# Decay sums of a gated linear attention: tokens on partitions and triangles on TensorE in place of scans on VectorE

## The chip, the core and the metric

The kernel runs on one core of a Trainium2 chip. The metric is the device time of one execution in microseconds; the number of a version is the median of its runs. The core has TensorE (matrix products, output to PSUM), VectorE, ScalarE and GpSimd for elementwise work, and a sync queue that issues most transfers. Each engine takes its instructions in a fixed order and waits at an instruction until its operands are there.

## The reference

One layer of a hybrid block: a modulated norm, one input projection for two groups of heads, an output projection and a SwiGLU feed-forward part. 2048 latent tokens and 256 context tokens, width 1024. The change is in group B, gated linear attention (GLA): 4 heads, 64 decay values a head, two directions. The decay of a token comes from a low-rank input of 16 values, a bias, a log-sigmoid and a division by 16; what the attention uses is its running sum within a chunk.

```python
loga = [log_sigmoid((glr[..., i * 16:(i + 1) * 16] @ g_gate_w[i] + g_gate_b[i])) / G_TAU for i in range(2)]
...
def step(S, inp):                                  # one chunk of gla_scan
    qc, kc, vc, ac = inp
    bcum = jnp.cumsum(ac, -2)                      # running sum of the decays
    decay = where(lower, bcum[..., :, None, :] - bcum[..., None, :, :], NEG)
    att = einsum('bhtk,bhsk,bhtsk->bhts', qc, kc, exp(decay))
    out = einsum('bhtk,bhkv->bhtv', qc * exp(bcum), S) + einsum('bhts,bhsv->bhtv', att, vc)
```

The second direction does the same on the flipped sequence. The kernel works with chunks of 128 tokens, for which the sums restart.

## The kernel before

**Stages.** All data are float32; most products are made in a fast float32 type (fp32r) with operands split in two parts. A main stream of units (projections: gates, keys and queries, values; then convolutions, output gates; then output projection and feed-forward part) is written out unit by unit. After each of its steps `after_step` advances the tasks: decays (`bt_task`, kind b), GLA (`scan_ga`, `state_g`, `scan_g`, kind g), mLSTM (`m_tables`, `state_m`, `scan_m`, kind m). A task is a generator; a `yield n` ends what it emits in this step.

**What sets the order.** For kinds b, g and m, tasks are advanced only while VectorE isn't more than a limit behind TensorE in a small model (`load.behind() > lim[0]`); it adds a fixed cost and a cost per column to each engine as instructions are emitted. A scheduler with its own timeline then fixes the order of each engine. A change of costs in one place so moves instructions elsewhere.

**A decay task.** `bt_task` handles 256 tokens for all four heads; there are nine (eight half blocks and the context). It loads the low-rank input three times (parts of a split), rounds it to fp32r (`glr`, 98 rows with the bias rows), and multiplies: for each head weights `w2[:, cs(h)]` are stationary and `glr` moves. The result `zh[h]` has 128 partitions (64 decays of the forward direction, 64 of the backward) and 256 tokens. Abs, Exp and Ln on ScalarE and a minimum-and-subtract on VectorE give the log-sigmoid. Two `tensor_tensor_scan` on VectorE for each head give the sums, on partitions 0 to 63 forwards and on 64 to 127 backwards, with a mask `rmask` that restarts the sum every 128 tokens. The result is stored to `d_bt` and loaded again by the GLA tasks, which turn it into factors (`dec` in `gla_e`, the levels in `gla_att`).

**Names.** `take()` hands out buffers of 128x256 named `arena`; `PS()` takes one of the four PSUM banks `ps`; `mm` are the four banks of the main stream; `gm` are five buffers of 128x512; `xall` holds the keys of the decay levels. `d_bg` and `d_mp` are small tables of `m_tables` that go through memory; `area` in ScalarE's rows of this stage is weight data of the modulation (`in_wada`).

## Time and profile before

| | us |
|---|---|
| median of 3 runs | 2954.2 (2951.46 to 2954.33) |
| profiled execution | 2949.42 |
| its span, first to last instruction | 2947.6 |
| TensorE busy | 2656.3 |
| VectorE busy | 1946.4 |
| GpSimd busy | 1781.4 |
| ScalarE busy | 1389.2 |

The mean granted clock of TensorE is 0.946 of full speed. The nine decay tasks run between 100 and 550 us, beside the input projections; the output projection and the feed-forward part follow from about 1400 us. Busy time is a mean over the span; the rows further down give it by stretches. A row's "idle before" and a wait name the operation that ended the idle time. Times in microseconds count from the start of the span.

### The profile page before, as it was taken

The numbers are of one execution on the slowest core, as the hardware profiler recorded it, in microseconds if no ns is written. First come the engines' busy times: TensorE is split into PE (matmuls) and PEld (weight loads), VectorE is DVE, ScalarE is ACT, GpSimd is POOL, SyncE is SP. The second block draws the span as 40 slices with busy tenths as digits, with TensorE's granted clock in tenths as the row PEclk, the third lists the DMA queues.
The fourth block names the chain that finished last, engine by engine and source line by source line (L and its number), as shares of the span: only waits on it lengthen the run. The fifth ranks groups of instructions, "written<-read, shape, count | busy, mean of one in ns | idle before, by whom it ended". The sixth has DMA issues, their size and how long they took to land. (4 is left out here: it accounts for less than half of the span.)

```text
span 2947.6 us, 43643 instructions
## 1 busy us (share of the span) xinstructions
PE 2656.3 (90%) x13322; PEld 2225.2 (75%) x13322; DVE 1946.4 (66%) x3949; ACT 1389.2 (47%) x3307; POOL 1781.4 (60%) x2339
## 2 busy tenths in 40 slices
PE   7889998698999977897999999889997999998898
PEld 4778887587777766775878888677786888886677
DVE  7678889886973435778778644767657444447775
ACT  4565555435455555655565433434434333333343
POOL 5767643345555534766767555777766655557773
PEclk8989899899999998997999999999998999999999
DMA  6755533246576776752443422422572432224222
GB/s 260 235 168 172 163 110 116 67 140 193 179 218 200 202 210 208 236 181 67 149 134 105 155 86 79 142 69 76 176 250 89 131 106 79 83 76 145 75 63 86
DMA packets 292458, 418.40 MB, mean 142 GB/s; under 512 B 38270, under 2 KB 176798, under 8 KB 289536
## 3 DMA queue, kind: packets, MB, share of 16 engines
q1 hardware_dynamic: 284864, 397.42, 43.4%
q0 software_dynamic: 7360, 18.19, 1.8%
q8 instruction: 106, 1.74, 0.3%
q14 instruction: 128, 1.05, 0.1%
HBM read 304.99 MB, written 110.49 MB: 141 GB/s over the span
## 5 line engine op out<-in xcount | busy, mean ns | idle before, releaser
L194 PE MATMUL mm<-area,w 128*128 128x512 f32 (+2 forms) x8264 | 1997.0, 399 | 119.2 <-DVE area L194 41.3
L194 PEld LDWEIGHTS mm<-area,w 128*128 128x128 f32 (+1 forms) x8264 | 1559.5, 193 | 465.2 <-DVE area L194 44.4
L194 POOL TENSOR_TENSOR w<-area,w 128x256 fp32r<-128x256 f32 x572 | 452.7, 814 | 295.6 <-ACT w L194 277.0
L194 POOL TENSOR_TENSOR w<-wr,w 128x256 fp32r<-128x256 f32 (+2 forms) x484 | 408.9, 865 | 205.7 <-ACT w L194 182.4
L194 POOL TENSOR_TENSOR arena<-arena 128x128 f32<-128x128 f32 (+1 forms) x520 | 245.5, 496 | 163.2 <-DMA arena<-d_bt 44.3
L194 ACT CAST w<-area 128x512 fp32r<-128x512 f32 x286 | 176.9, 620 | 285.7 <-PE mm L194 259.8
L194 PE MATMUL ps<-arena,arena 128*128 128x129 f32 (+1 forms) x1420 | 214.0, 292 | 58.8 <-ACT arena L194 29.5
L194 PEld LDWEIGHTS ps<-arena,arena 128*128 128x128 f32 x1420 | 193.6, 203 | 82.7 <-ACT arena L194 37.9
L194 PE MATMUL mm<-w,area 128*128 128x256 f32 x1728 | 245.6, 299 | 6.0 <-ACT gm L194 4.7
L194 DVE SCALAR_TENSOR_TENSOR gm<-gm,pc 128x63 f32<-128x63 f32 (+5 forms) x408 | 233.0, 613 | 7.2 <-ACT gm L194 4.8
L194 DVE TENSOR_TENSOR area<-area 128x512 f32<-128x512 f32 (+2 forms) x230 | 169.2, 749 | 100.6 <-DMA area<-in_wgu_dram 52.5
L194 PEld LDWEIGHTS mm<-w,area 128*128 128x128 f32 x1728 | 229.9, 204 | 7.7 <-ACT gm L194 4.9
L194 ACT CAST w<-wr 128x512 fp32r<-128x512 f32 (+3 forms) x272 | 158.1, 584 | 143.7 <-PE mm L194 62.9
L194 DVE TENSOR_TENSOR arena<-ps,arena 64x128 f32<-64x128 f32 (+1 forms) x512 | 154.9, 303 | 81.4 <-ACT ps L194 56.3
L194 DVE TENSOR_TENSOR gm<-mm,gm 128x512 f32<-128x512 f32 (+3 forms) x136 | 93.1, 684 | 159.0 <-PE mm L194 137.4
L194 ACT COPY gm<-mm 128x512 f32<-128x512 f32 (+3 forms) x215 | 123.2, 575 | 148.5 <-PE mm L194 128.1
L194 DVE SCALAR_TENSOR_TENSOR area<-mm,modc,area 128x512 f32<-128x512 f32 (+1 forms) x184 | 132.0, 722 | 92.0 <-PE mm L194 91.8
L194 ACT ACTIVATE ps<-arena 128x256 f32<-128x256 f32 x224 | 84.8, 383 | 157.4 <-DVE xall L194 106.4
L194 DVE TENSOR_TENSOR arena<-arena,arena 128x256 f32<-128x256 f32 (+2 forms) x146 | 117.1, 812 | 57.5 <-ACT arena L194 36.9
L194 PEld LDWEIGHTS ps<-arena,xall 128*128 128x128 f32 x896 | 125.6, 209 | 38.1 <-DVE arena L194 10.8
L194 PE MATMUL ps<-arena,xall 128*128 128x64 f32 x896 | 131.6, 289 | 24.4 <-DVE arena L194 13.1
L194 DVE TENSOR_TENSOR xall<-ps,arena 64x128 f32<-64x128 f32 x448 | 129.3, 289 | 6.9
(177 smaller groups left out, 3083.0 us busy)
## 6 DMA issues: line engine op xcount, KB each, us to landing
area<-in_wgu_dram SPq DMA_DIRECT2D x170, 256.0 KB, 2.7
d_ff<-gm SPq DMA_DIRECT2D x88, 256.0 KB, 2.0
arena<-d_ff SPq DMA_DIRECT2D x88, 256.0 KB, 2.8
wr<-in_win_dram SPq DMA_DIRECT2D x72, 256.0 KB, 3.6
area<-in_wada_dram SPq DMA_DIRECT2D x32, 512.0 KB, 4.6
wr<-in_wout_dram SPq DMA_DIRECT2D x64, 256.0 KB, 3.6
arena<-d_kq SPq DMA_DIRECT2D x112, 128.0 KB, 2.9
arena<-d_bt SPq DMA_DIRECT2D x80, 128.0 KB, 3.3
```

What stands on the lines that cost most here:

```text
L194: return f(out, *args, **kw)
```

## The change

The projection has its operands exchanged: a chunk of 128 tokens of `glr` is stationary and all 512 columns of `w2` move, so tokens stand on partitions and decays in columns. Abs, Exp, Ln and the subtraction are the same in number and shape. After one more step (`YB3`), each chunk, head and direction has a product with a triangle of ones: the 64 decays are stationary (128 tokens by 64), the triangle `tri` moves, and the output is again decays by tokens, 64x128, for the backward direction in partitions 64 to 127 and with -1. These products are in full float32. ScalarE copies the sums out of PSUM. The mask's place is taken by the two triangles.

```diff
-YB, YB2, YN, YGB = 1, 1, 1, 1
+YB, YB2, YB3, YN, YGB = 1, 1, 1, 1, 1
...
-    rm = np.ones((P, HB), np.float32)
-    rm[:, ::P] = 0
-    o["rmask"] = rm
+    o["tri"] = np.concatenate([np.triu(np.ones((P, P), np.float32)), -np.tril(np.ones((P, P), np.float32))], 1)
...
-    rmask = take()
-    dma(rmask, I["rmask"])
+    tri = take()
+    dma(tri, I["tri"])
...
         zs = [PS() for _ in range(2)]
-        for h in range(NH):
-            PE.matmul(zs[h // 2][:, h % 2 * HB:h % 2 * HB + HB], w2[:, cs(h)], glr, start=True, stop=True)
+        for c in range(2):
+            PE.matmul(zs[c], glr[:, cs(c)], w2, start=True, stop=True)
         ms = [take() for h in range(NH)]
-        zh = [zs[h // 2][:, h % 2 * HB:h % 2 * HB + HB] for h in range(NH)]
+        zh = [zs[i // 2][:, i % 2 * HB:i % 2 * HB + HB] for i in range(NH)]
...
         for h in range(NH):
-            m = o = ms[h]
-            V.scalar_tensor_tensor(m, zh[h], 0.0, m, ALU.min, ALU.subtract)
-            V.tensor_tensor_scan(o[0:64], rmask[0:64], m[0:64], 0.0, ALU.mult, ALU.add)
-            V.tensor_tensor_scan(o[64:128][:, ::-1], rmask[64:128], m[64:128][:, ::-1], 0.0, ALU.mult, ALU.subtract)
+            V.scalar_tensor_tensor(ms[h], zh[h], 0.0, ms[h], ALU.min, ALU.subtract)
+        yield YB3
+        os = [PS() for _ in range(2)]
+        for h in range(NH):
+            for c in range(2):
+                for d in range(2):
+                    PE.matmul(os[h // 2][64 * d:64 * d + 64, h % 2 * HB + c * P:h % 2 * HB + c * P + P],
+                              ms[2 * c + h // 2][:, h % 2 * P + 64 * d:h % 2 * P + 64 * d + 64], tri[:, cs(d)], start=True, stop=True)
+        free(*ms)
+        for h in range(NH):
+            o = take()
+            S.copy(o, os[h // 2][:, h % 2 * HB:h % 2 * HB + HB])
             dma(dst(h), o)
             free(o)
```

The order of the instructions changes too, and not only inside the tasks. On TensorE, at the second decay task, the projection was in four products (output `ps`, moving `gm`, weights `arena_329` as printed: output, then operands), between projections of keys and queries (`mm`):

```order
L194 MATMUL ps<-gm,arena_329 128x256 x2
L194 MATMUL mm<-area_471,w 128x512 x2
L194 MATMUL mm<-area_472,w 128x512 x12
L194 MATMUL mm<-area_553,w 128x512 x5
L194 MATMUL ps<-gm,arena_329 128x256 x2
L194 MATMUL ps<-arena_89,xall 128x64 x4
L194 MATMUL mm<-area_553,w 128x512 x7
L194 MATMUL mm<-area_554,w 128x512 x9
L194 MATMUL ps<-ones,area_814 128x2
```

and is now, in two products, followed by main stream and then by the first of the task's sixteen triangles (`arena_81` is `tri`, `arena_93` and `arena_94` are the decays):

```order
L192 MATMUL ps<-ones,area_814 128x2
L192 MATMUL ps<-arena_329,gm 128x512 x2
L192 MATMUL ps<-arena_91,xall 128x64 x4
L192 MATMUL mm<-area_297,w 128x256 x23
L192 MATMUL mm<-area_471,w 128x512 x12
L192 MATMUL mm<-area_472,w 128x512
L192 MATMUL ps<-ones,area_814 128x2
L192 MATMUL mm<-area_472,w 128x512 x11
L192 MATMUL mm<-area_553,w 128x512 x6
L192 MATMUL ps<-ones,area_814 128x2
L192 MATMUL mm<-area_553,w 128x512 x3
L192 MATMUL ps<-arena_81,arena_93 64x128 x2
```

The projection has become half as many products of twice the width; 56 products of the main stream and a level (`xall`) stand between it and the first triangle, and seven more pairs of triangles follow that row, of arena_94 and arena_93 in turn.

On VectorE, at the same task, the four subtractions (output and operands 128x256) and the scans (64x256, printed with the same operation's name; `arena_81` is the mask) were:

```order
L194 SCALAR_TENSOR_TENSOR arena_91<-ps,arena_91 128x256 x2
L194 SCALAR_TENSOR_TENSOR arena_91<-arena_81,arena_91 64x256 x2
L194 SCALAR_TENSOR_TENSOR arena_92<-ps,arena_92 128x256
L194 SCALAR_TENSOR_TENSOR arena_91<-arena_81,arena_91 64x256 x2
L194 SCALAR_TENSOR_TENSOR arena_92<-ps,arena_92 128x256
L194 TENSOR_SCALAR modc<-ps,pc 128x2
L194 TENSOR_TENSOR area_814<-area_814 128x256
L194 TENSOR_TENSOR arena_94<-ps,arena_88 64x128 x2
L194 SCALAR_TENSOR_TENSOR arena_92<-arena_81,arena_92 64x256 x2
L194 TENSOR_TENSOR xall<-ps,arena_87 64x32x4 x2
```

and are now:

```order
L192 TENSOR_TENSOR arena_95<-ps,arena_90 64x128 x2
L192 TENSOR_TENSOR xall<-ps,arena_89 64x16x8 x2
L192 SCALAR_TENSOR_TENSOR arena_93<-ps,arena_93 128x256
L192 TENSOR_TENSOR area_814<-area_814 128x128
L192 SCALAR_TENSOR_TENSOR arena_93<-ps,arena_93 128x256
L192 SCALAR_TENSOR_TENSOR arena_94<-ps,arena_94 128x256 x2
L192 TENSOR_SCALAR modc<-ps,pc 128x2
L192 TENSOR_TENSOR area_814<-area_814 128x256
L192 TENSOR_TENSOR area_814<-area_814 128x128
```

The eight scans of the task are gone; the additions of the modulation weights (`area_814`) and the multiplications of the levels (`xall`) come closer together.

On the sync queue, at the small table `d_bg` of `m_tables`, the order was:

```order
L210 DMA d_bt<-arena_85 128x256 x2
L208 DMA arena_85<-d_kq 128x256
L210 DMA d_bg<-sm_6006 128x2x1
L208 DMA arena_89<-d_bt 128x256
L208 DMA arena_90<-d_bg 4x2x16 x2
L210 DMA d_qT<-gm 128x512
L210 DMA d_mp<-arena_90 4x2x16 x2
L208 DMA sm_6024<-d_mp 128x2x1
L208 DMA mpb<-d_mp 128x128
```

and is now:

```order
L208 DMA d_kq<-gm 64x2x256
L208 DMA d_bg<-sm_6128 128x2x1
L208 DMA d_kq<-gm 64x2x256 x2
L206 DMA arena_82<-d_bg 4x2x16 x2
L208 DMA d_kq<-gm 64x2x256
L206 DMA arena_95<-d_gv 128x256
L206 DMA arena_86<-d_us 64x256
L208 DMA d_kq<-gm 64x2x256 x2
L208 DMA d_att<-arena_83 128x256
L208 DMA d_mp<-arena_82 4x2x16
```

The load of decays (`d_bt`) that stood between the store and the loads of `d_bg` has moved ahead of this place; stores of keys and queries (`d_kq`) and loads for the GLA state (`d_gv`, `d_us`) stand there instead, and the table comes at a later state of GLA.

## Rows read from the trace of the kernel before

**Rows 1.** The page, section 1: busy time, share of the span, instructions

```profile
span 2947.6 us, 43643 instructions
...
PE 2656.3 (90%) x13322; PEld 2225.2 (75%) x13322; DVE 1946.4 (66%) x3949; ACT 1389.2 (47%) x3307; POOL 1781.4 (60%) x2339
```

**Rows 2.** Busy time by stretches; columns: stretch, length, engines, clock, DMA

```profile
core 0: us, PE busy (x) PEld busy (x) DVE busy (x) ACT busy (x) POOL busy (x), PEclk, DMA share, GB/s
...
100.00:300.00 200.00, 175.40 (x1174) 164.01 (x1172) 155.63 (x385) 121.25 (x306) 147.08 (x208) 0.91 0.59 186
300.00:400.00 100.00, 90.69 (x614) 83.79 (x615) 86.22 (x229) 57.28 (x129) 56.87 (x106) 0.88 0.50 153
400.00:550.00 150.00, 137.44 (x804) 121.41 (x803) 132.34 (x309) 82.93 (x177) 58.84 (x100) 0.97 0.34 103
...
860.00:1100.00 240.00, 216.22 (x1125) 180.11 (x1124) 89.55 (x262) 119.68 (x387) 120.93 (x194) 0.97 0.70 206
```

**Rows 3.** Groups of VectorE: count, busy us, mean ns, idle before

```profile
L194 DVE TENSOR_TENSOR_SCAN arena<-arena,arena 64x256 f32<-64x256 f32 x70 | 60.0, 857 | 0.8
L194 DVE TENSOR_TENSOR_SCAN arena<-arena 64x256 f32<-64x256 f32 x2 | 1.4, 703 | 0.0
```

**Rows 4.** TensorE's waits, 100 to 300 us: total, times, longest us

```profile
PE ps L194 <- DVE arena L194: 7.5, 4, 3.7
...
PE ps L194 <- DVE xall L194: 2.1, 4, 0.8
...
PE ps L194 <- DVE gm L194: 1.2, 1, 1.2
```

**Rows 5.** TensorE's waits, 300 to 400 us

```profile
PE ps L194 <- DVE arena L194: 4.0, 2, 2.5
PE mm L194 <- DVE area L194: 3.6, 2, 3.3
...
PE ps L194 <- DVE gm L194: 0.6, 1, 0.6
```

**Rows 6.** TensorE's waits, 400 to 550 us

```profile
PE ps L194 <- DVE xall L194: 5.4, 4, 2.4
PE mm L194 <- ACT gm L194: 4.7, 1, 4.7
```

**Rows 7.** Timeline of all engines, 553 to 567 us: start, us, engine, instruction

```profile
553.38 0.37 SPq L210 DMA_DIRECT2D d_bg<-sm  x1
...
553.84 0.42 SPq L208 DMA_DIRECT2D arena<-d_bt  x1
...
562.87 0.66 SPq L208 DMA_DIRECT2D arena<-d_bg  x2
...
565.93 0.42 ACT L194 ACTIVATE dec<-arena 64x2 f32<-64x2 f32 x2 [10.48 <-DMA arena<-d_bt]
...
566.21 0.24 DVE L194 TENSOR_TENSOR_SCAN arena<-arena,mctx 4x16 f32<-4x16 f32 x1 [9.45 <-DMA arena<-d_bg]
...
566.96 0.58 ACT L194 COPY gm<-mm 128x512 f32<-128x512 f32 x1
567.12 7.82 PE L194 MATMUL mm<-area,w 128*128 128x512 f32 x24 [15.54 <-ACT gm L194]
```

**Rows 8.** Groups of TensorE over the whole span

```profile
L194 PE MATMUL mm<-area,w 128*128 128x512 f32 x7992 | 1946.1, 401 | 109.4 <-DVE area L194 37.7 <-ACT gm L194 20.1 <-ACT area L194 18.3
...
L194 PE MATMUL mm<-w,area 128*128 128x256 f32 x1728 | 245.6, 299 | 6.0 <-ACT gm L194 4.7 <-POOL w L194 1.2
...
L194 PE MATMUL ps<-gm,arena 98*128 98x256 f32 x36 | 6.8, 296 | 2.4 <-DVE gm L194 2.0 <-DVE xall L194 0.3
```

**Rows 9.** Groups of TensorE: the products of the decay levels

```profile
L194 PE MATMUL ps<-arena,xall 128*128 128x64 f32 x896 | 131.6, 289 | 24.4 <-DVE arena L194 13.1 <-DVE xall L194 8.4 <-DVE gm L194 1.5
```

**Rows 10.** Timeline of TensorE, 1011 to 1015 us

```profile
1011.45 2.40 PE L194 MATMUL ps<-arena,arena 128*128 128x129 f32 x20
1013.61 1.41 PE L194 MATMUL mm<-area,w 128*128 128x512 f32 x5
```

**Rows 11.** Groups of TensorE, 100 to 300 us

```profile
L194 PE MATMUL ps<-arena,xall 128*128 128x64 f32 x172 | 27.0, 303 | 4.1 <-DVE arena L194 2.7 <-DVE xall L194 1.0
```

**Rows 12.** Groups of TensorE, 400 to 550 us

```profile
L194 PE MATMUL ps<-arena,xall 128*128 128x64 f32 x116 | 16.0, 274 | 6.1 <-DVE xall L194 5.4 <-DVE arena L194 0.4 <-issue 0.3
```

**Rows 13.** Groups of ScalarE over the whole span

```profile
L194 ACT ACT_TABLE_LOAD x33 | 42.3, 1283 | 1.3 <-PEq L2149 0.7
...
L194 ACT COPY arena<-ps 128x256 f32<-128x256 f32 x104 | 37.9, 370 | 21.9 <-DVE arena L194 15.7 <-PE ps L194 6.0
```

**Rows 14.** Timeline of ScalarE, 226 to 234 us

```profile
226.42 0.65 ACT L194 ACTIVATE arena<-ps 128x256 f32<-128x256 f32 x2
226.95 1.27 ACT L194 ACTIVATE area<-area,cx 128x128 f32<-128x128 f32 x4
...
230.39 0.42 ACT L194 ACTIVATE arena<-arena 128x256 f32<-128x256 f32 x1
230.83 1.28 ACT L194 ACT_TABLE_LOAD   x1
232.13 0.73 ACT L194 ACTIVATE arena<-arena 128x256 f32<-128x256 f32 x2
...
233.01 0.72 ACT L194 ACTIVATE arena<-arena 128x256 f32<-128x256 f32 x2
```

**Rows 15.** Busy time by stretches of 20 us (columns as in rows 2)

```profile
460.00:480.00 20.00, 14.10 (x105) 13.76 (x103) 19.63 (x37) 5.28 (x11) 11.65 (x19) 0.91 0.53 157
```

**Rows 16.** ScalarE's waits, 100 to 300 us

```profile
ACT area L194 <- DMA area<-in_wada_dram: 29.5, 15, 4.0
```

More of the change, by code (lines that the diff above doesn't have):

```diff
@@ L153 @@
     wout=(KT, P, KT, P), wgu=(2 * FT, P, KT, P), wdown=(6, P, KT, P), wd6=(8, P, 12, P), wd4=(4, P, 8, P), pc=(P, NPC), w2=(98, NH * P),
-    ident=(P, P), mneg=(P, 2, P), lmask=(P, len(LEVELS) * 128), rmask=(P, HB))
+    ident=(P, P), mneg=(P, 2, P), lmask=(P, len(LEVELS) * 128), tri=(P, 2 * P))
 class Task:
```

## The prediction

> **What bounds the kernel now.** I read the busy line first [rows 1]: TensorE is busy 2656.3 of 2947.6 us (90%), VectorE 1946.4 (66%). Such a mean hides the stages, so next the table by stretches [rows 2]. The decays are made by nine tasks (eight half blocks and the context), and their scans [rows 3] fall between 100 and 300 us (five tasks) and 400 and 550 us (four). In these stretches and the one between, both engines are close to full: TensorE 175.4 of 200, 90.7 of 100 and 137.4 of 150 us, VectorE 155.6, 86.2 and 132.3. The reader should compare this with the stretch 860 to 1100, where VectorE has next to nothing to do (89.6 of 240) and TensorE is still busy for only 216.2 of 240, again 90%. So a tenth of idle TensorE is what this program shows with a free VectorE too; relieving VectorE doesn't make TensorE's products disappear. Every product that is added has to be paid somewhere unless it falls into a wait.
>
> Which waits are there is in the lists of TensorE's waits. Between 100 and 300 those put down to VectorE are 7.5 + 2.1 + 1.2 = 10.8 us [rows 4], between 300 and 400 4.0 + 3.6 + 0.6 = 8.2 us [rows 5], between 400 and 550 5.4 us, and 4.7 behind ScalarE's copies, which wait for VectorE's convolution [rows 6]. Together 29 us. Behind them comes one large hole: TensorE stands 15.5 us up to 567.1 [rows 7].
>
> **The change, part by part.** All sums are against the profiled execution, 2949.4 us (its span is 2947.6); the median of the runs shown, 2954.2, lies 4.8 above it, and I add that at the end.
>
> Scans. 72 are removed, 60.0 + 1.4 = 61.4 us of VectorE [rows 3]. The minimum-and-subtract stays. By itself this is worth only what TensorE waits for VectorE.
>
> Projection. 36 products of 256 columns go (6.8 us, [rows 8]); 18 of 512 columns come, at 1946.1 / 7992 = 0.244 us each like the kernel's other ones of that type, 4.4 us. Net -2.4 us.
>
> Sums by triangles. Per task 16 products in full float32 with 64 weight columns and 128 moving ones; 144 in all. The trace writes a full float32 product as two records: the decay levels have 7 levels x 2 chunks x 32 tasks = 448 products and 896 records [rows 9]. So 288 records are added. No row of before has 64 weight columns. From below: a dense row of 20 records with 129 moving columns runs from 1011.45 to the next row's start at 1013.61, 0.108 us each [rows 10], 31.1 us for 288. From above: in the two stretches themselves, where the clock is lower and the products stand among others, such records cost 27.0 / 172 = 0.157 and 16.0 / 116 = 0.138 us [rows 11, 12], so 160 x 0.157 + 128 x 0.138 = 42.8 us. I take the middle, 37. TensorE's net addition is 37 - 2.4 = 35 us.
>
> Copies. 36 copies of 128x256 from PSUM, 37.9 / 104 = 0.364 us each, 13.1 us of ScalarE; the new order also holds 27 table loads where it had 33, so 6 x 1.283 = 7.7 us go [rows 13]. Net +5.4 us on an engine that is busy 121 of 200 and 83 of 150 us in these stretches [rows 2]: nothing, and if a later copy of the main stream waits for them, at most these 5 us. The 36 stores of the decays on the sync queue are the same in number and size, only behind the copy instead of the scan, and the constant that is loaded is as large as the mask it replaces: nothing.
>
> A new wait. The products with triangles stand in TensorE's queue behind Abs, Exp, Ln and the subtraction. That chain took 7.3 us in the trace, from 226.4 to 233.7 [rows 14]. In the new order 23 products of 256 columns and 33 of 512 lie between a task's projection and its first triangle: 23 x 245.6 / 1728 + 33 x 0.244 = 11.3 us [rows 8]. That covers the chain, so I take nothing; what a hole costs is in the third rival, and behind a standing product everything of the main stream would wait.
>
> What comes back. (a) Of the 29 us of waits for VectorE I let a third go, 10 us: VectorE falls from 83% busy in 100 to 550 to about 70%, not to nothing, and most of these waits are single chains a few us long that start from one producer. (b) The hole before 567 us [rows 7]: the sync queue issues the tiny-element store of d_bg at 553.4, right behind it a load of decays, and stands until 562.9; ScalarE waits 10.5 us for that load at its factor dec, and the copies that free TensorE's banks are behind it. In the new order no load of decays follows that store; stores of keys and queries and later loads do. VectorE's wait for d_bg itself (9.5 us) stays. I let half of the hole go, 8 us. (c) The clock: 0.91 and 0.88 between 100 and 400 us [rows 2] means about 60 of these 300 us at 1.2 GHz instead of 2.4, worth 30 us at most if TensorE had work throughout. With more products and fewer holes I let a sixth come back, 5 us.
>
> Sum: 35 - 10 - 8 - 5 = +12 us, 2961 in the profile, 2966 as a median. Its own range, with 31 to 43 for the triangles and 15 to 28 given back: +1 to +25, 2955 to 2979.
>
> **The rivals.**
> First, VectorE sets the pace up to 560 us, and the change makes the kernel faster. For it: between 460 and 480 us VectorE is busy 19.6 of 20 us and TensorE 14.1 [rows 15]; and TensorE's waits before a level's product are for VectorE's multiplications, which come late in their queue; the decay tasks put 6.8 us of scans in front of it each. Against it: TensorE's 90% with an idle VectorE. Then all 29 us go, the whole hole of 15.5, and half of the clock's 30: 35 - 60 = -25, 2929 as a median. It decides from the point where more than 35 of these 75 us come back.
>
> Second, the triangles are cheaper than any row says, since two neighbours write the two halves of the output partitions and need only half of the array each; if such neighbours run side by side, 288 records cost half, 18.5 us, and the sum is 16 - 23 = -7, 2947: at the edge of no change. For it is the new order, where the two directions alternate; against it, that no row of before shows products side by side. The Trainium skill states this rule (TensorE: Matmul & The Clock Gate, the part on packing small matmuls by row and column tiling): products in different column tiles of the array overlap, and three with 32 columns ran 2.38 times as fast. No run here shows it.
>
> Third, the wait that I cost at nothing. The chain's 7.3 us was that of one task; ScalarE also waits for loads of modulation weights, 29.5 us between 100 and 300 [rows 16], each task now asks twice for two of the four PSUM banks of its pool, and VectorE's subtractions stand among other work. With 3 us of standing in each of nine tasks the sum is 12 + 27 = +39, 2993.
>
> **How the numbers follow.** The forecast has 0.47, the first rival 0.22, the second 0.15, the third 0.16. A measurement of this kernel can tell about 0.2%, 6 us, from no change. Faster than that: nearly all of the first rival, half of the second and the edge of the forecast, 0.31. Within it: the rest of the second and the forecast's lower end, 0.17. Slower: 0.52. For 8 in 10 the range reaches from below the first rival to above the third, 2924 to 2997; the forecast's own is the one above.
>
> **What would show it.** The scans over 64x256 inside the tasks are gone and VectorE's total falls by about 60 us. A group of 288 records 64 columns wide appears; 31 to 43 us of busy time in it speak for the forecast, under 20 for the second rival. TensorE's total rises by about 35 us less what the clock gives back. Waits of TensorE before these products on ScalarE or VectorE above 20 us in all are the third rival. If the point at which 550 us stood before is reached over 10 us earlier, the first rival holds. If the hole at d_bg stays as long, my term (b) is wrong; if the clock from 100 to 400 stays at 0.9, term (c) is. The forecast as a whole is wrong if the decay tasks' stretches together get shorter.

## The result, and the profile after

The changed kernel takes 2903.4 us (median of four runs, 2900.2 to 2911.68) against 2953.3 (four runs) for the kernel before on the same chip: ratio 0.9842, interval 0.9821 to 0.9862, faster by about 50 us. Two more sets of runs on other chips gave 0.9833 and 0.9833 (below). The forecast was 2966, and no time in its range of 2924 to 2997 was this low. Since chips differ by up to half a per cent, experiments are compared by their ratio to the kernel before on the same chip.

The profiled execution took 2911.68 us, at the upper end of the runs. The page's span and busy line of the changed kernel, to [rows 1]:

```profile
span 2909.9 us, 44224 instructions
...
PE 2651.0 (91%) x13592; PEld 2218.3 (76%) x13592; DVE 1893.2 (65%) x3877; ACT 1394.0 (48%) x3337; POOL 1762.2 (61%) x2339
```

TensorE has 270 more records and is busy 5 us less. The span is 37.7 us shorter, so 32 us of idle TensorE went. Busy time by stretches of the changed kernel: the four of [rows 2] first, and then two of a second kind:

```profile
100.00:300.00 200.00, 179.97 (x1341) 166.06 (x1340) 130.34 (x377) 128.27 (x336) 144.72 (x223) 0.96 0.62 194
300.00:400.00 100.00, 91.77 (x688) 84.95 (x687) 82.84 (x222) 60.67 (x141) 54.19 (x106) 0.98 0.53 153
400.00:550.00 150.00, 142.26 (x888) 123.69 (x887) 124.58 (x295) 79.75 (x185) 59.46 (x102) 0.98 0.35 108
...
860.00:1100.00 240.00, 217.11 (x1143) 182.93 (x1143) 95.33 (x286) 130.00 (x426) 113.03 (x184) 0.95 0.70 206
...
124.34:550.36 426.02, 393.43 (x2752) 355.08 (x2751) 324.60 (x871) 253.21 (x623) 245.11 (x416) 0.97 0.48 147
1056.28:1130.72 74.44, 69.22 (x379) 58.06 (x378) 43.53 (x137) 48.40 (x150) 42.51 (x60) 0.98 0.80 233
```

Stretches of equal clock time hold different work in two kernels. The products of the main stream (output `mm`) help: they are 10,360 records in every kernel here, so the n-th of them is the same place of the work. I cut there: A from record 400 to 2200 (all nine decay tasks lie in it or just before), B to 3800, C to 4000, D to 5400. C is where the main stream of the projections is over and the program asks for what is left of the tasks; I call it the barrier. The last two lines above are A and C of the changed kernel; the same two of the kernel before:

```profile
122.80:576.54 453.74, 393.11 (x2465) 357.14 (x2463) 377.50 (x936) 249.76 (x582) 254.76 (x406) 0.90 0.45 136
1057.46:1175.49 118.03, 90.04 (x453) 76.86 (x452) 56.45 (x167) 64.41 (x212) 53.43 (x79) 0.84 0.72 213
```

In A TensorE does 287 more records in the same busy time (393.11 and 393.43), since the granted clock is 0.97 where it was 0.90, and its idle time falls from 453.74 - 393.11 = 60.6 to 32.6 us. Not all of these 28.0 us are won: the hole at `d_bg` [rows 7], 15.54 us, lies in A before, and in the changed kernel it comes behind record 2200, in B, where it is 7.50 us long (below). A and B together have 91.7 us of idle time where they had 111.0. In C TensorE has 74 records less to do, because tasks ran earlier, and 5.2 us of idle time where there were 28.0. The lengths of all stretches, from the same view (us; the last column is the rest, up to the last of these records):

| kernel | A | B | C | D | rest |
|---|---|---|---|---|---|
| before | 453.7 | 480.9 | 118.0 | 529.2 | 1225 |
| changed | 426.0 | 505.9 | 74.4 | 536.5 | 1226 |
| changed, third set of runs | 419.8 | 496.8 | 73.7 | 531.9 | 1225 |
| changed, scans added (e1) | 451.8 | 506.2 | 84.4 | 532.0 | 1226 |
| before without scans (e17) | 421.7 | 474.7 | 115.7 | 521.0 | 1225 |
| before, new plan (e14) | 448.2 | 510.0 | 78.9 | 520.9 | 1227 |
| neither, new plan (e13) | 423.3 | 504.9 | 75.8 | 537.9 | 1225 |
| neither, new plan (e16) | 428.0 | 499.7 | 84.6 | 529.8 | 1225 |
| changed, old account (e4) | 414.3 | 486.8 | 167.5 | 513.4 | 1226 |

The changed kernel wins 28 us in A, gives 25 back in B, where 48 more records of the tasks now stand (2419 for 2371, and 446.79 us busy for 430.54) and the hole with them, wins 44 at the barrier and gives 7 back in D. In this execution, the slowest of its four, nothing of the lead is left at the end of B: record 3800 is reached at 1056.3 us, where it was 1057.5. In the profiles of the two other sets it is reached at 1040.2 and 1039.7.

The table takes the gain apart. Without scans, in the old plan (e17), A is short and the barrier is as long as before; with the scans, in the new plan (e14), A is long and the barrier is short, and B longer by 29 us. With the scans beside the changed work (e1) A is as long as before and the barrier stays short. So what is won in A goes with the scans, and what moves from C to B goes with the plan.

The groups that the change added or touched, TensorE first (to [rows 3, 8]), then ScalarE (to [rows 13]):

```profile
L192 PE MATMUL mm<-w,area 128*128 128x256 f32 x1728 | 235.5, 291 | 1.7 <-POOL w L192 0.9 <-ACT w L192 0.6 <-ACT gm L192 0.2
L192 PE MATMUL ps<-arena,arena 128*64 128x128 f32 x272 | 21.1, 298 | 6.5 <-DVE arena L192 3.5 <-ACT arena L192 1.6 <-DVE xall L192 1.3
L192 PE MATMUL ps<-arena,gm 98*128 98x512 f32 x18 | 7.0, 443 | 3.3 <-DVE gm L192 3.3
L192 PE MATMUL ps<-arena 128*64 128x128 f32 x16 | 1.5, 271 | 0.0
```

```profile
L192 ACT COPY arena<-ps 128x256 f32<-128x256 f32 x140 | 49.2, 370 | 34.8 <-DVE arena L192 23.9 <-issue 6.1 <-PE ps L192 4.5
L192 ACT ACT_TABLE_LOAD x27 | 34.6, 1283 | 2.2 <-DVE arena L192 1.0 <-PEq L2157 0.7
```

The 288 records of the triangles took 22.6 us, and TensorE stood 6.5 us ahead of them in all. The waits of TensorE from 400 to 550 us (to [rows 6]) are small now, and the hole at `d_bg` (to [rows 7]), here in the timeline of all engines, has shrunk:

```profile
PE ps L192 <- DVE arena L192: 3.0, 4, 2.1
PE ps L192 <- DVE gm L192: 1.8, 2, 1.1
PE ps L192 <- ACT arena L192: 1.6, 1, 1.6
PE ps L192 <- DVE xall L192: 1.3, 2, 1.0
```

```profile
571.80 0.37 SPq L208 DMA_DIRECT2D d_bg<-sm  x1
...
582.15 0.63 SPq L206 DMA_DIRECT2D arena<-d_bg  x2
583.49 0.24 DVE L192 TENSOR_TENSOR_SCAN arena<-arena,mctx 4x16 f32<-4x16 f32 x1 [6.42 <-DMA arena<-d_bg]
...
585.48 0.69 ACT L192 ACTIVATE gm<-mm,kqs 128x512 f32<-128x512 f32 x1 [13.99 <-DMA d_kq<-gm]
...
587.00 1.22 PE L192 MATMUL ps<-arena,arena 128*128 128x128 f32 x4 [7.50 <-ACT arena L192]
```

The load that reads `d_bg` back still comes 10.35 us behind its store; TensorE's wait there is 7.50 us where it was 15.54. No load of decays stands behind the store any more, but ScalarE's row at 585.48 waited 13.99 us for a store of keys and queries (`d_kq`) that does.

### The profile page after: what moved, and what is told of

It is laid out like the page before. It is cut to its first block, busy times and chain, and to the rows that moved or that the text cites. A ratio compares the mean times of both kernels' runs of the same rounds, so it can differ in the third digit from the quotient of the medians.

```text
span 2909.9 us, 44224 instructions
## 1 busy us (share of the span) xinstructions
PE 2651.0 (91%) x13592; PEld 2218.3 (76%) x13592; DVE 1893.2 (65%) x3877; ACT 1394.0 (48%) x3337; POOL 1762.2 (61%) x2339
## 5 line engine op out<-in xcount | busy, mean ns | idle before, releaser
L192 PEld LDWEIGHTS mm<-area,w 128*128 128x128 f32 (+1 forms) x8264 | 1556.5, 193 | 448.2 <-DVE area L192 53.2
L192 POOL TENSOR_TENSOR w<-wr,w 128x256 fp32r<-128x256 f32 (+2 forms) x484 | 390.3, 826 | 167.9 <-ACT w L192 138.7
L192 PE MATMUL ps<-arena,arena 128*128 128x129 f32 (+2 forms) x1676 | 236.8, 296 | 70.0 <-ACT arena L192 27.4
L192 PEld LDWEIGHTS ps<-arena,arena 128*128 128x128 f32 (+1 forms) x1676 | 210.9, 195 | 99.0 <-ACT arena L192 37.2
L192 DVE SCALAR_TENSOR_TENSOR gm<-gm,pc 128x441 f32<-128x441 f32 (+5 forms) x408 | 234.0, 617 | 11.7 <-ACT gm L192 9.5
L192 PE MATMUL mm<-w,area 128*128 128x256 f32 x1728 | 235.5, 291 | 1.7 <-POOL w L192 0.9
L192 PEld LDWEIGHTS mm<-w,area 128*128 128x128 f32 x1728 | 220.0, 195 | 4.4 <-POOL w L192 1.1
L192 DVE TENSOR_TENSOR arena<-arena,arena 128x256 f32<-128x256 f32 (+4 forms) x147 | 117.6, 810 | 61.5 <-ACT arena L192 35.3
L192 PEld LDWEIGHTS ps<-arena,xall 128*128 128x128 f32 x896 | 117.0, 197 | 26.3 <-issue 10.3
L192 PE MATMUL ps<-arena,xall 128*128 128x64 f32 x896 | 120.7, 276 | 17.0 <-DVE sm L192 6.1
```

The source lines that it names most:

```text
L192: return f(out, *args, **kw)
```

## The experiments

**Names.** The account is the small model `load` by which tasks are held back; the plan is the list of which task takes its next step at which step of the main stream. The account decides the plan: with the triangles added and the scans gone it sees VectorE less far behind, and the tasks start earlier (the last step of the last `state_m` is at main step 121, before at 124; the barrier is at 133). `V.` and `PE.` report to the account, `nc.vector.` and `nc.tensor.` don't; so work and plan can be changed apart. The order inside an engine is fixed after that by the scheduler's timeline and can still differ under one plan.

**e1: the scans again, beside the changed work, unknown to the account (same plan).** Their output is thrown away.

```diff
+            j = take()
+            nc.vector.tensor_tensor_scan(j[0:64], tri[0:64], ms[h][0:64], 0.0, ALU.mult, ALU.add)
+            nc.vector.tensor_tensor_scan(j[64:128][:, ::-1], tri[64:128], ms[h][64:128][:, ::-1], 0.0, ALU.mult, ALU.subtract)
+            free(j)
```

> The changed kernel with the 72 scans put back on VectorE as idle work (their results are stored in a buffer that nothing reads; the emission model is not told of them). Theory R (the relief of VectorE pays): the 61 us of scans take back 35 to 50 us, 2938 to 2953. Theory O (the new interleaving of tasks pays, which the model sets): the gain stays, 2900 to 2915. Theory C (only the low price of the triangles let it pay, together with R): as R.

Measured 2943.8 us, ratio 0.998 (0.9969 to 0.9991). Nearly the whole gain is gone, with triangles, layout and plan in place. Its windows of A and C:

```profile
124.42:576.22 451.80, 400.92 (x2749) 359.42 (x2747) 380.95 (x927) 255.22 (x621) 258.51 (x417) 0.95 0.46 137
1082.37:1166.80 84.43, 73.84 (x401) 61.31 (x400) 47.32 (x150) 53.18 (x166) 45.69 (x63) 0.96 0.73 221
```

VectorE has 56 us more in A than in the changed kernel, and A is 26 us longer: 18 us more of idle TensorE, and 7 us more of busy time at a lower clock (0.95, not 0.97). Part of it comes from where the added scans stand, among the subtractions that the triangles need; TensorE now stands 16.7 us ahead of the triangles, where it stood 6.5:

```profile
L192 PE MATMUL ps<-arena,arena 128*64 128x128 f32 x280 | 22.1, 299 | 16.7 <-DVE arena L192 12.4 <-DVE xall L192 4.2
```

GpSimd's busy time moves with the scans as well: 1788.7 us in e1, 1762.2 in the changed kernel and 1781.4 before, with 2339 instructions each time. No run separates what this is worth from VectorE's own relief.

**e2: before, without scans, plan of before.** The running sums are left out; the backward half is only negated, by 36 operations of VectorE (14.5 us).

```diff
-            V.tensor_tensor_scan(o[0:64], rmask[0:64], m[0:64], 0.0, ALU.mult, ALU.add)
-            V.tensor_tensor_scan(o[64:128][:, ::-1], rmask[64:128], m[64:128][:, ::-1], 0.0, ALU.mult, ALU.subtract)
+            nc.vector.tensor_scalar(o[64:128], m[64:128], -1.0, None, ALU.mult)
+            load.add("V", o, ())
+            load.add("V", o, ())
```

> The kernel before without its scans: the running sums are left out (the backward half is only negated, one small VectorE instruction per head), and the emission model is still told of the scans' cost. No triangles. R: faster than the changed kernel, since the relief comes without the triangles, 2880 to 2903. O: little, 2940 to 2953.

Measured 2907.1, ratio 0.9856 (0.9836 to 0.9876), a little slower than the first range. The same relief is worth the same 1.4% in the old plan, without triangles.

**e3: before's work with the changed account.**

```diff
-            V.tensor_tensor_scan(o[0:64], rmask[0:64], m[0:64], 0.0, ALU.mult, ALU.add)
-            V.tensor_tensor_scan(o[64:128][:, ::-1], rmask[64:128], m[64:128][:, ::-1], 0.0, ALU.mult, ALU.subtract)
+            nc.vector.tensor_tensor_scan(o[0:64], rmask[0:64], m[0:64], 0.0, ALU.mult, ALU.add)
+            nc.vector.tensor_tensor_scan(o[64:128][:, ::-1], rmask[64:128], m[64:128][:, ::-1], 0.0, ALU.mult, ALU.subtract)
+            load.t["PE"] += 4 * P * 4 / 2400
```

> The kernel before, unchanged in its work, but the emission model is not told of the scans and is told of the triangles' TensorE time, so tasks are advanced as in the changed kernel. R: no gain, 2945 to 2965. O: most of the gain, 2905 to 2925.

Measured 2961.25, ratio 1.0027 (1.0014 to 1.004). This earlier plan (last `state_m` at step 115) alone gives nothing.

**e4: the changed work with the account of before.**

```diff
             V.scalar_tensor_tensor(ms[h], zh[h], 0.0, ms[h], ALU.min, ALU.subtract)
+            load.add("V", ms[h], ())
+            load.add("V", ms[h], ())
...
-                    PE.matmul(os[h // 2][64 * d:64 * d + 64, h % 2 * HB + c * P:h % 2 * HB + c * P + P],
+                    nc.tensor.matmul(os[h // 2][64 * d:64 * d + 64, h % 2 * HB + c * P:h % 2 * HB + c * P + P],
```

> The changed kernel, unchanged in its work, but the emission model is told of scans that aren't there and not of the triangles, so tasks are advanced by the old costs. R: the gain stays, 2895 to 2915. O: it is lost, 2940 to 2955.

Measured 2954.3, ratio 1.0022 (1.0008 to 1.0037): the theory by which relief alone makes the gain fell here. The work is the changed kernel's, and the whole gain is gone. The place is the barrier. Its window there, and the first two of TensorE's waits in it:

```profile
1024.99:1192.50 167.51, 117.02 (x639) 99.39 (x638) 71.53 (x239) 99.85 (x348) 69.82 (x108) 0.84 0.74 214
```

```profile
PE ps L192 <- ACT arena L192: 26.0, 10, 8.1
PE ps L192 <- DVE arena L192: 18.4, 12, 4.7
```

Five tasks are unfinished at the barrier in this plan (none in the changed kernel's), 260 more records have to be done there, and TensorE waits for their short chains with nothing of the main stream to fill in. A was even shorter, 414.3 us, though with one task's triangles less in it (256 of the 288 records). VectorE's time is free, but the plan doesn't use it. This plan isn't the one of before: the old account is charged for the scans and each decay task is a step longer, so the last `state_m` ends at step 130, where it ended at 124. No run has the changed work in the very plan of before; e11 (step 125) comes nearest.

**e5: the triangles ordered by half.** The expectations of e5 to e8 are in microseconds of a chip on which the kernel before takes 2953; on theirs it takes 2939.5, so they are read by the ratio. All forward products (output partitions 0 to 63) of a task come first, then all backward ones.

```diff
-        for h in range(NH):
-            for c in range(2):
-                for d in range(2):
+        for d in range(2):
+            for h in range(NH):
+                for c in range(2):
```

> The changed kernel with the triangle products in another order: all of the forward half (output partitions 0 to 63) first, then all of the backward half, so that neighbours write the same half. In the changed kernel a dense run of 28 records took 1.75 us, 0.063 each. Theory S (neighbours in different halves run side by side): a dense record takes about 0.108 us, and TensorE has 11 to 13 us more to do. Theory W (a record of 64 weight columns is shorter by itself, since less weight is loaded): 0.06 to 0.07 as before, and the time stays at 2903 within 8 us.

One task's triangles in TensorE's timeline, first of the changed kernel, then of e5, and e5's group:

```profile
168.10 2.08 PE L192 MATMUL ps<-arena,arena 128*64 128x128 f32 x32
```

```profile
163.99 3.33 PE L192 MATMUL ps<-arena,arena 128*64 128x128 f32 x32
```

```profile
L192 PE MATMUL ps<-arena,arena 128*64 128x128 f32 x272 | 33.2, 287 | 5.1 <-DVE arena L192 2.1 <-DVE xall L192 1.7 <-ACT arena L192 1.4
L192 PE MATMUL ps<-arena 128*64 128x128 f32 x16 | 3.0, 272 | 0.0
```

The same 32 records take 0.104 us each when neighbours write the same half and 0.065 when they alternate; all of them 36.2 against 22.6 us. So neighbours in different halves do run side by side. The time: 2895.1, ratio 0.985 (0.9835 to 0.9865), within 0.2% of the changed kernel. So S holds for the records and W's time came true, because the 13.6 us more of triangles cost only 2 to 5 us by the ratios. At 36 us, about what I had forecast for the triangles, the kernel still gains 1.5%.

**e6: every triangle twice, same plan.** The account isn't told of the second product.

```diff
                     PE.matmul(os[h // 2][64 * d:64 * d + 64, h % 2 * HB + c * P:h % 2 * HB + c * P + P],
                               ms[2 * c + h // 2][:, h % 2 * P + 64 * d:h % 2 * P + 64 * d + 64], tri[:, cs(d)], start=True, stop=True)
+                    nc.tensor.matmul(os[h // 2][64 * d:64 * d + 64, h % 2 * HB + c * P:h % 2 * HB + c * P + P],
+                              ms[2 * c + h // 2][:, h % 2 * P + 64 * d:h % 2 * P + 64 * d + 64], tri[:, cs(d)], start=True, stop=True)
```

> The changed kernel with each triangle product made twice, to the same place (the emission model is told of one), so about 22 us more on TensorE and nothing more on VectorE. If TensorE has no room in these stretches: 15 to 25 us slower than the changed kernel, 2918 to 2928. If the products fall into waits and a clock that rises with them: at most 6 us slower, 2900 to 2910.

Measured 2911.0, ratio 0.9902 (0.9885 to 0.9918): 0.5% above e5 on the same chip, 0.6 to 0.7% above the changed kernel. In the timeline a task's 64 records stand from 168.45 to 172.52 us, 2 us longer than its 32, some 18 us for nine tasks; the time is 15 to 20 us longer by the medians. As far as the intervals tell, a second set is paid in full.

**e7: e4 with a wider limit. e8: the changed kernel with a wider limit.** The limit is how far VectorE may be behind by the account before tasks are held back.

```diff
-LIM, LIM2, PACED = 8.0, 5.0, 'bgm'
+LIM, LIM2, PACED = 16.0, 5.0, 'bgm'
```

```diff
-LIM, LIM2, PACED = 8.0, 5.0, 'bgm'
+LIM, LIM2, PACED = 10.0, 5.0, 'bgm'
```

> The run in which the changed kernel was paced by the old costs (2954.3 us), with one number changed: tasks may be advanced while VectorE is up to 16 behind TensorE in the model, not 8. By the plan of the emission the last state task then ends at step 117 (130 without it, 121 in the changed kernel), and no task is left over where the main stream ends (5 without it). Theory P (how far the tasks are ahead when the main stream ends decides): the loss goes, 2895 to 2915. If the old costs hurt in another way: 2940 to 2955.

> The changed kernel with the limit at 10 in place of 8; by the plan the last state task ends at step 117 in place of 121. P: further ahead is better still, 2885 to 2900. If what is ahead at 8 is enough: 2897 to 2910. If VectorE has no more room for it: above 2910.

e7 0.9912 (0.9897 to 0.9928), between the two ranges (2927 us on the first chip): 1.1 of the 1.8% that e4 lost are back, with C at 87.9 us and nothing left at the barrier. e8 0.9913 (0.9894 to 0.9933), the third case: earlier still is not better, 0.7% worse. Both plans end their last `state_m` at step 117, and the two times agree.

**e9 to e12, on one chip.** e9 is e2's work (running sums left out) with the changed account (first diff). e10 is the changed kernel. e11 is the changed kernel with the scans reported to the account (the first two added lines of e4). e12 is the changed kernel without the pause (second diff).

```diff
             nc.vector.tensor_scalar(o[64:128], m[64:128], -1.0, None, ALU.mult)
-            load.add("V", o, ())
-            load.add("V", o, ())
+            load.t["PE"] += 4 * P * 4 / 2400
```

```diff
-        yield YB3
```

> The kernel before without its 72 scans (the running sums are left out; the backward half is only negated) and without the triangles, but with the changed kernel's account of the work, so that the steps are started as early as there. Theory P (the gain has two parts, VectorE's relief and steps that run ahead): this has both and not the price of the triangles and copies, which the doubled triangles put at about 17 us; so it is faster than the changed kernel by 0.3 to 0.7%, that is a ratio of 0.977 to 0.981 to the kernel before (2885 to 2898 us against 2953). Rival Q (only the relief counts, and steps further ahead are worth nothing): as without scans and with the old account, ratio 0.984 to 0.987 (2906 to 2915 us).

> The changed kernel itself, beside the others on one chip: ratio 0.982 to 0.987 to the kernel before by every theory. It is the measure for the three others of this call.

> The changed kernel's work; the account is told of the triangles, and of 72 scans as well that are no longer there. By the account no step is then left for the point where the main stream of the projections ends (with the old account 5 were). Theory P1 (what counts is that nothing is left there): within 0.3% of the changed kernel, 0.983 to 0.988 (2903 to 2918 us). Rival P2 (each step that starts later costs, whether left over or not): half of what the old account lost, 0.991 to 0.996 (2927 to 2941 us).

> The changed kernel without the new pause between VectorE's last operation on the decays and the triangles, so each of the 18 steps is one step shorter and TensorE reaches the first triangle sooner behind VectorE. If steps further ahead are worth something (theory P): faster than the changed kernel by 0.1 to 0.4%, ratio 0.980 to 0.983. If the pause covers a wait (rival W): 18 waits of 1 to 2 us on TensorE come instead, 18 to 36 us, ratio 0.990 to 0.997; the row of the triangles would show them as idle time ahead, ended by VectorE.

e9 0.9845 (0.9829 to 0.9861), e10 0.9833 (0.9821 to 0.9846). The first theory of e9 falls, and Q's range is met: without triangles and with early steps it is no faster than the changed kernel. e11 0.9917 (0.9903 to 0.993), in the range of P2: no task is left at its barrier by the plan, yet C is 115.2 us long, so "nothing left over" is not the whole rule. e12 0.9922 (0.9907 to 0.9938): the time is the one given for W, but the mechanism isn't; TensorE's idle time ahead of the triangles is 4.9 us, less than with the pause. A is 454.0 us there, and three waits in it, which A of the changed kernel hasn't, come to 24.8 us: the hole at `d_bg` (9.1, here ahead of record 2200), one of 7.7 behind other work of VectorE, and one of 8.04 behind a single addition of VectorE to the modulation weights:

```profile
188.46 7.43 DVE L192 TENSOR_TENSOR area<-area 128x256 f32<-128x256 f32 x1
196.69 0.56 PE L192 MATMUL ps<-ones,area 128*128 128x2 f32 x2 [8.04 <-DVE area L192]
```

Another such addition in e12 took 8.74 us. Each kernel has 32 of this shape, with medians of 0.42 to 0.65 us; the longest in the three profiles of the changed kernel took 1.31.

**e13 to e15: which part is the plan?** e13 is e2's work (sums left out), e14 the work of before with its scans, both with the changed account and the pause, so that all steps of all tasks stand where they do in the changed kernel. e15 moves the pause ahead of VectorE's last operation on the decays; the order on TensorE is the same row for row.

```diff
             V.scalar_tensor_tensor(m, zh[h], 0.0, m, ALU.min, ALU.subtract)
+        yield YB3
```

```diff
+        for h in range(NH):
+            load.add("V", ms[h], ())
+        yield YB3
         for h in range(NH):
-            V.scalar_tensor_tensor(ms[h], zh[h], 0.0, ms[h], ALU.min, ALU.subtract)
-        yield YB3
+            nc.vector.scalar_tensor_tensor(ms[h], zh[h], 0.0, ms[h], ALU.min, ALU.subtract)
```

> The kernel before without its 72 scans (running sums left out, the backward half only negated), without triangles, with the changed kernel's account and with its added pause, so that every step of every task starts and ends at the same place of the plan as in the changed kernel. Theory O (the plan with the pause is worth about 0.9% by itself, as the kernel without the pause suggests): 0.974 to 0.979 to the kernel before. Rival C (the pause is worth something only because it keeps the triangles' wait off TensorE): as without the pause, 0.982 to 0.987. Read with the changed kernel (0.983 to 0.984) it gives the price of triangles and copies in one plan: 0.5 to 0.9% by O, nothing by C.

> The work of the kernel before, scans and all, and no triangles, in the plan of the changed kernel (its account and its pause). Theory O: 1.003 for that work without the pause, less 0.9%, so 0.991 to 0.996 (2927 to 2941 us). Rival C: 1.000 to 1.005. Against the kernel without scans in the same plan it is the third price of VectorE's 61 us: 1.2 to 1.8% by both.

> The changed kernel with the pause moved from behind VectorE's last operation on the decays to just ahead of it (36 minimum-and-subtracts now stand directly ahead of the triangles); the order on TensorE is the same row for row, and so is the plan. Theory O (the plan counts): 0.982 to 0.988. Rival C (the pause keeps the wait for this VectorE operation off TensorE): 0.988 to 0.994, and waits for VectorE of 10 to 30 us in all stand ahead of the triangles in TensorE's rows (6.5 us in the changed kernel).

e13 0.9893 (0.9875 to 0.9911), e14 0.9958 (0.9945 to 0.9972), e15 0.9836 (0.9822 to 0.9851). e15 settles that the pause covers no wait for VectorE's last operation: its triangles,

```profile
L192 PE MATMUL ps<-arena,arena 128*64 128x128 f32 x272 | 20.4, 291 | 5.4 <-DVE arena L731 3.0 <-ACT arena L192 1.6 <-DVE xall L192 0.8
```

wait 5.4 us, and the time is the changed kernel's. e13 misses both ranges: it has neither scans nor triangles, and is slower than the changed kernel. e14 lies in O's range, but its distance to e13 is 0.65%, and both theories had 1.2 to 1.8% for it.

**e16 to e18: is e13 slow because of its sign operations?** As e13 and e2, with the negation on ScalarE (sums left out); e18 is the changed kernel on the same chip.

```diff
-            nc.vector.tensor_scalar(o[64:128], m[64:128], -1.0, None, ALU.mult)
+            nc.scalar.activation(o[64:128], m[64:128], AF.Copy, scale=-1.0)
```

> As the run without scans and triangles in the changed kernel's plan, but the sign of the backward half, which stood on VectorE with 36 operations of 17.1 us in all, is made by 36 operations of ScalarE. So all 61 us of scans are off VectorE. Theory V (VectorE's microseconds are worth 0.02 to 0.03% each while the main stream runs; the triangles themselves cost TensorE little, since they fall into its waits): 0.982 to 0.986, level with the changed kernel within 0.3%. Rival W (those 17 us are off the path, and work without triangles is slower for another reason): as with the sign on VectorE, 0.988 to 0.991. Theory O of before, in which the triangles cost 0.5% and more: 0.974 to 0.980.

> The same in the kernel before: its own account and plan, no scans, no triangles, the sign on ScalarE. With the sign on VectorE (14.5 us) the ratio was 0.9856. Theory V: another 0.3 to 0.45%, 0.981 to 0.983. Rival W: 0.985 to 0.987.

> The changed kernel, beside the two others on one chip: 0.982 to 0.985 by every theory. It is the measure for the first of them.

e16 0.9883 (0.9865 to 0.9902), e17 0.986 (0.9845 to 0.9874), e18 0.9833 (0.9818 to 0.9848). Rival W's times are met: moving these 15 to 17 us from VectorE to ScalarE gains nothing in either plan. Whether they are worth nothing isn't shown by that, since ScalarE takes 13.1 us for them in e16, which also has four table loads more than e13. Windows of A, e16 and then e18:

```profile
125.33:553.32 427.99, 378.65 (x2480) 344.14 (x2479) 333.50 (x864) 267.44 (x629) 244.97 (x418) 0.94 0.46 145
```

```profile
123.09:542.87 419.78, 389.59 (x2752) 352.90 (x2751) 324.05 (x871) 253.24 (x623) 246.69 (x416) 0.97 0.47 148
```

With 272 records fewer, e16 has 49.3 us of idle TensorE in A against 30.2. Two waits behind VectorE make up most of the difference, 8.29 and 7.63 us; A of e18 has none above 5. Ahead of the first, one addition of VectorE took 10.70 us:

```profile
153.83 10.70 DVE L194 TENSOR_TENSOR area<-area 128x256 f32<-128x256 f32 x1
165.44 0.56 PE L194 MATMUL ps<-ones,area 128*128 128x2 f32 x2 [8.29 <-DVE area L194]
496.56 1.12 PE L194 MATMUL ps<-arena,xall 128*128 128x64 f32 x4 [7.63 <-DVE xall L194]
```

e13 has no addition as long as that and loses its time in B and D (by the table), so this is not the whole reason.

**The two factors in the changed plan**, ratios to before:

| | scans on VectorE | no scans |
|---|---|---|
| no triangles | 0.9958 (e14) | 0.9883 (e16), 0.9893 (e13) |
| triangles and the new layout | 0.998 (e1) | 0.9842, 0.9833, 0.9833 (changed) |

Taking the scans off is worth 0.65 to 0.75% above and 1.4% below; in the old plan 1.4% (e2, e17). The triangles and the layout cost 0.2% beside the scans, and without them the kernel with triangles is the faster one, by 0.5%. The whole work of the change is worth 1.2% in this plan (e14 to the changed kernel) and 1.0% in the plan without the pause (e3 to e12); the plan by itself is worth 0.4% (before to e14).

## Why the prediction was wrong

**The step that failed is "What comes back", 23 us: above all its term (c), 5 us for the clock, and a term that the sum doesn't have, the barrier.** Over the whole span TensorE got 22.8 us of new work (triangles 22.6, projection 0.2). Its idle time fell by 32.4 us, and its busy time fell by 5.3 although the 22.8 were added, so 28.1 us came back there: 22.8 - 32.4 - 28.1 = -37.7, the difference of the spans, where I had 35 - 18 - 5 = +12. In A alone the 22.8 us were done in an unchanged busy time (393.11 and 393.43) at a clock of 0.97 in place of 0.90, so some 22 us came back with the clock where (c) had 5. My "sixth" of 30 us was a choice with no row behind it. The idle terms (a) and (b) were nearly right where they were meant: 18 forecast, and 111.0 - 91.7 = 19.3 us in A and B together, since the hole of (b) moved from A to B. At the barrier, for which I had no term, another 22.8 us of idle time went.

The relief shows the same without any triangle. In A of e17 (before without scans, old plan)

```profile
124.03:545.75 421.72, 378.18 (x2452) 343.80 (x2451) 321.68 (x860) 263.57 (x615) 239.39 (x402) 0.94 0.47 145
```

TensorE is busy 14.9 us less than before, at 0.94, and idle 17.1 us less (6.8 of these at the hole, which is 8.7 us long there). By the ratios the relief by itself is worth 0.65 to 1.4%, 19 to 42 us (e1, e2, e17, and e14 with e13 and e16).

**The premise under it.** I argued that a tenth of idle TensorE is there with a free VectorE too, from 860 to 1100 us [rows 2], and let that stand for a floor. As a share it is nearly one: in A TensorE went from 86.6% busy (393.11 of 453.74) to 92.3%. But a busy share doesn't say how much is done in a busy microsecond. The stretch that I read it from ran at 0.97 already, and A at 0.90; that was the larger part of what could come back, and I took 5 us for it.

**Triangles: 37 us forecast, 22.6 measured.** The second rival's mechanism is true, and e5 shows it. The Trainium skill (TensorE: Matmul & The Clock Gate, Part 3) says that products in different tiles of the array overlap, and that the output's start partition is the column tile; the rows agree, with 36.2 / 22.6 = 1.6 for two halves in full float32. But it didn't decide: e5 takes this gain away and stays at 0.985. So the size of this term was wrong by 14 us, and the sign of the forecast was not lost by it.

**Point by point.** Scans: their rows are gone, but VectorE's total fell by 53.2 us, not 61.4. Projection: 7.0 us for 18 products, 0.39 each, where I took 0.244 from another group; +0.2 instead of -2.4. Copies: 49.2 - 37.9 = 11.3 us (13.1 forecast); six table loads less, as read. The new wait at nothing: right, 6.5 us in all, and e15 shows that the cover of the last VectorE operation wasn't even needed (the 7.3 us that I read in [rows 14] are ScalarE's part of the chain, without that operation). (a): TensorE's waits for VectorE from 400 to 550 us are 6.1 us (5.4 before), and those for ScalarE 1.6 (4.7); in the lists of all three stretches what answers to the 29 us is about 20, so the third that I let go is right. In A as a whole the waits for VectorE fell from 25.0 to 18.7 us, those for ScalarE from 23.7 to 5.0 (the hole among them), and those for GpSimd, of which I had none, from 10.1 to 4.0. (b): 15.54 to 7.50 us, 8.0 as forecast; the load of decays is gone as I read it, but the half was a guess, and its hit is luck. (c): the clock from 100 to 400 us is 0.96 and 0.98; the test was met, the size four times too small.

**The rivals.** The first had the right sign, and A bears out its mechanism in part: relieving VectorE shortens that stretch. Its time, 2929, used 35 us for the triangles; with 22.8 in place of 35 it would have given 2917. What came back over the span, 60.5 us, is its 60, but not part by part: it had 15 for the clock and nothing for the barrier, so the agreement is in part luck. My test of it decides less than I meant. The point of 550 us is record 2172 of the main stream; the changed kernel reaches it at 541.9 us in this profile, 8 us earlier, and at 533.9 and 532.7 in the profiles of the other two sets, on either side of the line of 10. (Record 2200 comes 26 us earlier, but 15.5 of these are the hole.) The sign that I gave for the forecast as a whole being wrong, shorter stretches of the decay tasks, is there: A is 28 us shorter, some 12 without the hole.

**What no case contained.** The account was told of the triangles and no longer of the scans, and I read that only as moved instructions. By itself the new plan is worth 0.4% (e14), and it makes the barrier short. With the old account and the longer tasks (e4) the same work gains nothing, because tasks are left for the barrier. Every other plan that I tried for the changed work is 0.7 to 1.9% slower than the changed kernel's own, to either side of it. By the step at which the last `state_m` ends: 115 in e12 (0.9922), 117 in e7 and e8 (0.9912, 0.9913), 121 in the changed kernel (0.983 to 0.984), 125 in e11 (0.9917), 130 in e4 (1.0022).

**Open.** Why the plan fits this work so well, and why, in this very plan, the kernel without triangles is slower by 0.5% (e13, e16). The profiles point at the order inside the engines and at single stretched additions of VectorE (10.70 us in e16, 8.74 and 7.43 in e12), of which the changed kernel's three profiles have none in A; no run keeps them away from the other kernels. Other candidates that no run took apart: the new layout's 27 table loads against 35 in e16 (31 in e13, which is no faster), and the clock (0.97 against 0.94 in A of e16). That the triangles "cost nothing" is not shown in general: a second set is paid (e6).

## What to carry to other kernels

Where two engines are both over 80% busy in one stretch, price the relief of the second by that stretch: idle time and clock come back together, and here the clock was nearly half of it. Before two stretches are compared, see whether one large wait has crossed their border. If a model paces the work, a change of costs is two changes, work and plan; test them apart, and look at the points where the program waits for everything, because what a plan leaves there costs as much as the work itself gains. After such a change a difference below 1% between two plans says little about the work.

## What was not expected of the hardware

Full float32 products with 64 weight columns took 0.104 us a record in the same half of the output partitions and 0.065 alternating between the halves (e5), against 0.108 with 128 weight columns [rows 10]: half the columns alone save next to nothing. And more products cost no busy time where the granted clock rose with them: 2752 records in 393.43 us at 0.97 against 2465 in 393.11 at 0.90. Third, a VectorE addition of 128x256 in float32, 0.42 to 0.65 us in the median, took 10.70 us in e16 and 8.74 and 7.43 in e12; GpSimd was busy for over 96% of each of the three. No run shows whether that is the cause.
